# Strassen's seven products for four of eight projection kinds in a decoder layer on one core

## The chip, the cores and the metric

The kernel runs on one core of a Trainium2 chip. The metric is the device time of one execution in microseconds, the median of several runs. The core's engines are TensorE (PE, with its weight loads as PEld), VectorE (DVE), ScalarE (ACT), GpSimd (POOL) and SyncE (SP), which here only issues DMAs. Each engine works through its own queue in order and waits on semaphores for the others.

## The reference

One layer on L = 272 tokens (16 meta tokens ahead of 256), width 4096, all in float32:

```python
h = rmsnorm(x, norm_g)
p = h @ w_in                        # 4096 x 16384: eight kinds q k v g b c h z, 16 units of 128 columns each
o = stick_breaking_attention(q, k, v)             # 16 heads of 128, strictly causal
o = group_rmsnorm(o * silu(g), attn_norm_g, 16)   # norm over the 128 channels of a head
y = b * short_conv(c * h, conv_w)                 # width 3 along the tokens
y = group_rmsnorm(y * silu(z), conv_norm_g, 16)
x = x + concat([o, y]) @ w_out                    # 4096 x 4096
return rmsnorm(x, final_norm_g)[:, 16:]
```

A weight a(t, s) of the attention is sigmoid(z_ts) times the product of (1 - sigmoid(z_tj)) over s < j < t; it is computed in log space with a running sum along the keys.

## The kernel before, in words

All of w_in and w_out is read once, as 640 chunks of 128 x 1024 float32 (512 KB). Each chunk is split into two float32r parts, so that three products (high x low, high x high, low x high) make up for the short mantissa: `split` casts the chunk on ScalarE to `wh` (line 87) and subtracts on VectorE for `wl` (line 88). x comes transposed (`xt`), is scaled by norm_g and split in the same way into `xs` (`prep_x`, lines 190 and 191) and stays in SBUF, 32 slices of k with a high and a low part side by side. The factor 1/rms of each token is applied after the projection (`rstd`).

The projection works by channel: a block is 128 output columns of one kind and unit; its weights are held still in TensorE and the tokens stream. `mm_k` does one k of a block. For k, v, c and h it takes three matmuls of 272 or 258 columns (lines 227 to 229). For q, g, b and z, which need only the 256 real tokens, it takes one matmul of 256 columns with `wl` (line 221) and one of 512 with `wh`, high and low part of x side by side (line 223; line 220 is that for the first k); the two halves of the bank are added afterwards by `fold`.

The order of the work is written out by hand in `steps`: the first four blocks interleaved over k while x arrives (16 chunks), then block after block, heads and conv units in turn, four chunks a block; then the output projection by columns, each step two token tiles (`mm_out`, lines 476 to 478, the mixed channels held still and the weights streaming). The loop issues loads four chunks ahead and splits three ahead (`LOADS, SPLITS`). Everything else (scores, weights, transposes by 32 x 32 blocks, the short convolution, SiLU, the group norm with its matmul by ones on lines 281 and 282, `norm_b`) is put on a list by `later` and issued a few steps behind its block. The mixed channels stay in SBUF, already split, from the end of a unit on. Each PSUM tile is a bank of a pool of eight.

Of the kernel before, what the change touches and what calls it, by code (L numbers as in the profile page):

```python
# [8 lines left out]
F32 = mybir.dt.float32  # L9
# [6 lines left out]
P = 128  # L16
D = 4096
# [4 lines left out]
XROW = 320  # L22
HEADS = 16
UNITS = 32
EPS = 1e-6
# [11 lines left out]
S0 = 7  # L37
# [6 lines left out]
def kernel(ctx, tc, xt, xin, par, fg, w1, w2, out):  # L44
    nc = tc.nc

    const = ctx.enter_context(tc.tile_pool(name="const", bufs=1))
    wp = ctx.enter_context(tc.tile_pool(name="wp", bufs=4))
    wk = ctx.enter_context(tc.tile_pool(name="wk", bufs=1))

    wp.tile([P, 16], F32, name="pad_w", bufs=1)
    pp = ctx.enter_context(tc.tile_pool(name="pp", bufs=8, space=bass.MemoryType.PSUM))

    def bank(nm):
        return pp.tile([P, 512], F32, tag="bank", name=nm)


    ones = const.tile([P, P], F32, name="ones")
# [9 lines left out]
    raws, splits = {}, {}  # L68

    def load(ci, parts=1):  # L70
        t = wp.tile([P, 1024], F32, tag="raw", name=f"raw{ci}", bufs=4)
        n = 1024 // parts
        for i in range(parts):
            nc.sync.dma_start(out=t[:, i * n:(i + 1) * n], in_=src_of(ci)[:, i * n:(i + 1) * n])
        raws[ci] = t

    def split(ci, parts=1):
        t = raws.pop(ci)
        if ci in keep:
            h, lo = keep[ci]  # L80
        else:
            h = wp.tile([P, 1024], F32R, tag="wh", name=f"wh{ci}", bufs=4)
            lo = wp.tile([P, 1024], F32R, tag="wl", name=f"wl{ci}", bufs=4)
        n = 1024 // parts
        for i in range(parts):
            c = slice(i * n, (i + 1) * n)
            nc.scalar.copy(out=h[:, c], in_=t[:, c])  # L87
            nc.vector.tensor_tensor(out=lo[:, c], in0=t[:, c], in1=h[:, c].bitcast(F32), op=ALU.subtract)  # L88
        splits[ci] = (h, lo)


    ones_r = const.tile([P, P], F32R, name="ones_r")
    nc.scalar.copy(out=ones_r, in_=ones)


    za = const.tile([P, 3 * P + 64], F32, name="za")
    nc.vector.memset(za[:, 3 * P:], 0.0)

    at = const.tile([P, META + 3 * P], F32, name="at")
    nc.vector.memset(at[:, :META], 0.0)  # L100
    vt = const.tile([P, L + META], F32, name="vt")
    nc.vector.memset(vt[:, L:], 0.0)
    zmask = const.tile([P, ZW], F32, name="zmask")
    nc.vector.memset(zmask, 0.0)
    for off in (META, 144 + META + P):

        nc.gpsimd.affine_select(out=zmask[:, off:off + P], in_=zmask[:, off:off + P],
                                pattern=[[-1, P]], compare_op=ALU.is_gt, fill=NEG,
                                base=0, channel_multiplier=1)
    one = const.tile([P, 1], F32, name="one")  # L110
    nc.vector.memset(one, 1.0)
    gsc = const.tile([P, 32], F32, name="gsc")
    nc.vector.tensor_scalar(out=gsc, in0=pt[:, AG0:AG0 + 32], scalar1=RS, scalar2=None, op0=ALU.mult)
    rstd = const.tile([P, L], F32, name="rstd")

    def rsqrt_raw(src, n, eps, nm):

        x = wk.tile([P, 272], F32, tag="rx", name=f"rx{nm}", bufs=1)[:, :n]
        y = wk.tile([P, 272], F32, tag="ry", name=f"ry{nm}", bufs=1)[:, :n]
        t = wk.tile([P, 272], F32, tag="rt", name=f"rt{nm}", bufs=1)[:, :n]  # L120
# [12 lines left out]


    mixh, mixl = [], []

    def open_mix():
        sctx.close()
        mixp = ctx.enter_context(tc.tile_pool(name="mixp", bufs=1))
        mixp.tile([P, 24], F32, name="pad_m")  # L140
        mixh.extend(mixp.tile([P, SEQ], F32R, name=f"mixh{m}") for m in range(UNITS))
        mixl.extend(mixp.tile([P, SEQ], F32R, name=f"mixl{m}") for m in range(UNITS))

    steps = [(0, kc) for kc in range(16)]
    for b in range(4, 128):
        steps.extend((b, kc) for kc in range(4))
    n1 = len(steps)

    for nb in range(7):
        steps.extend((128 + nb, kc) for kc in range(16))
    for nb in (7, 8):
        steps.extend((128 + nb, kc) for kc in range(8))
    n_steps = len(steps)
    keep = {}

    def src_of(ci):
        return w1[ci] if ci < n1 else w2[ci - n1]

    LOADS, SPLITS = 4, 3
    tasks = []

    def later(at, fn):
        tasks.append((at, fn))

    def run_tasks(i):
        ready = [t for t in tasks if t[0] <= i]
        for t in ready:
            tasks.remove(t)  # L170
        for t in ready:
            t[1]()
# [7 lines left out]
    xr = [sp.tile([P, 4, L], F32, name=f"xr{j}") for j in range(8)]  # L180
    xsum = sp.tile([P, L], F32, name="xsum")

    def load_x(k, n):
        j, kk = k // 4, k % 4
        nc.sync.dma_start(out=xr[j][:, kk:kk + n, :], in_=xt[:, k:k + n, :])

    def prep_x(k):
        j, kk = k // 4, k % 4
        g = pt[:, G0 + k:G0 + k + 1]
        nc.scalar.mul(out=xs[j][:, kk, 0, :L], in_=xr[j][:, kk, :], mul=g)  # L190
        nc.vector.scalar_tensor_tensor(out=xs[j][:, kk, 1, :L], in0=xr[j][:, kk, :], scalar=g,
                                       in1=xs[j][:, kk, 0, :L].bitcast(F32),
                                       op0=ALU.mult, op1=ALU.subtract)

    def stat_x(j):
        tc.keep_in_program_order(nc.scalar.square(out=xr[j], in_=xr[j]))
        xq = sp.tile([P, L], F32, tag="xq", name=f"xq{j}", bufs=2) if j else xsum
        tc.keep_in_program_order(
            nc.vector.tensor_reduce(out=xq, in_=xr[j].rearrange("p k t -> p t k"), axis=AX.X, op=ALU.add))
        if j:  # L200
            nc.vector.tensor_tensor(out=xsum, in0=xsum, in1=xq, op=ALU.add)

    def finish_stats():
        ss = bank("ss_x")
        nc.tensor.matmul(out=ss[:, :L], lhsT=ones, rhs=xsum, start=True, stop=True)
        xm = wk.tile([P, 272], F32, tag="sg", name="xm")
        nc.vector.tensor_scalar(out=xm, in0=ss[:, :L], scalar1=1.0 / 32.0, scalar2=None, op0=ALU.mult)
        u = rsqrt_raw(xm, L, EPS, "x")
        nc.vector.tensor_scalar(out=rstd, in0=u, scalar1=RS, scalar2=None, op0=ALU.mult)
# [3 lines left out]
    def mm_k(b, k, h, lo):  # L213

        ps = psum[b]
        x = xs[k // 4][:, k % 4, :, :L]
        first, last = k == 0, k == KC - 1
        if b % 8 in (0, 3, 6, 7):
            if first:
                nc.tensor.matmul(out=ps, lhsT=h, rhs=x[:, :, META:], start=True, stop=False)  # L220
            nc.tensor.matmul(out=ps[:, :SEQ], lhsT=lo, rhs=x[:, 0, META:], start=False, stop=False)  # L221
            if not first:
                nc.tensor.matmul(out=ps, lhsT=h, rhs=x[:, :, META:], start=False, stop=last)  # L223
        else:
            s = 0 if b % 8 < 4 else META - 2
            o = ps[:, s:L]
            nc.tensor.matmul(out=o, lhsT=h, rhs=x[:, 0, s:], start=first, stop=False)  # L227
            nc.tensor.matmul(out=o, lhsT=h, rhs=x[:, 1, s:], start=False, stop=False)  # L228
            nc.tensor.matmul(out=o, lhsT=lo, rhs=x[:, 0, s:], start=False, stop=last)  # L229

    def mm_in(ci):
        b, kc = steps[ci]
        wh, wl = splits.pop(ci)
        if kc == 0:
            for bb in range(b, b + 4 if b == 0 else b + 1):
                psum[bb] = bank(f"mm{bb}")
        for kk in range(8):
            h = wh[:, kk * P:(kk + 1) * P]
            lo = wl[:, kk * P:(kk + 1) * P]
            if b == 0:  # L240
                mm_k(kk % 4, 2 * kc + kk // 4, h, lo)
            else:
                mm_k(b, kc * 8 + kk, h, lo)

    def blocks(dst, src, n):

        d = dst.rearrange("p (c x) -> p c x", c=n)
        s = src.rearrange("p (c x) -> p c x", c=n)
        for i in range(4):
            for j in range(4):  # L250
                o = d[32 * j:32 * j + 32, :, 32 * i:32 * i + 32]
                x = s[32 * i:32 * i + 32, :, 32 * j:32 * j + 32]
                if (i + j) % 2:
                    nc.vector.tensor_copy(out=o, in_=x)
                else:
                    nc.scalar.copy(out=o, in_=x)  # L256

    def fold(ps, r, nm, tag, width=SEQ):

        t = wk.tile([P, width], F32, tag=tag, name=f"{tag}{nm}")[:, :SEQ]  # L260
        nc.scalar.copy(out=t, in_=ps[:, SEQ:])
# [376 lines left out]
```

## Time and profile before

| | us |
|---|---|
| median of 3 runs | 1874.1 (1874.07 to 1874.17) |
| the profiled execution | 1873.31 |
| its span, first to last instruction | 1871.5 |
| granted TensorE clock in it | 0.998 |
| PE / DVE / ACT / POOL busy | 1859.1 / 1224.7 / 953.6 / 0.7 |

Busy time is the union of an engine's instructions. A row of a group reads: line, engine, operation, what is written and read, shapes, count | total busy us, mean ns of one | idle us of the engine just before them, and what ended that idle time. TensorE's matmuls overlap, so their means are longer than the distance from one to the next. A row of the timeline reads: start us, duration us, engine, line, operation. A row of the stretches gives for each engine its busy us with the count of instructions, then the granted clock, the DMA share and GB/s. A row of the waits reads: who waited for whom, us in total, times, longest us.

### The profile page before, as it was taken

How to read it: one execution, taken by the hardware profiler on the slowest of the kernel's cores; microseconds unless marked ns; L12 is line 12 of the kernel's file. 1: busy time of each engine (PE TensorE's matmuls, PEld its weight loads, DVE VectorE, ACT ScalarE, POOL GpSimd, SP SyncE). 2: the span in 40 equal slices, each digit the busy share in tenths (PEclk: the TensorE clock that was granted, in tenths of full speed). 3: DMA queues.
4: the chain of work that ended last, by engine and by line, in shares of the span. 5: the costliest groups of instructions: out<-in, count | busy, mean ns of one | idle time of the engine just before them, and what ended most of it. 6: DMA issues, size and time to landing. Idle time of an engine off the chain costs nothing.

```text
span 1871.5 us, 30516 instructions
## 1 busy us (share of the span) xinstructions
PE 1859.1 (99%) x12214; PEld 1707.0 (91%) x12214; DVE 1224.7 (65%) x1904; ACT 953.6 (51%) x1381; POOL 0.7 (0%) x6
## 2 busy tenths in 40 slices
PE   9999999999999999999999999999999999999997
PEld 8999999999999999999999999999999988888887
DVE  8987676767676767676767676767676765555544
ACT  7665555545454545454545454545454544444443
POOL 0000000000000000000000000000000000000000
PEclk9999999999999999999999999999999999999999
DMA  8555555555555555555555555555555586566564
GB/s 310 179 182 181 177 184 175 186 172 189 171 188 172 186 174 184 177 183 178 181 180 181 180 181 180 181 180 180 181 179 182 175 285 207 198 197 200 198 201 162
DMA packets 100510, 352.53 MB, mean 188 GB/s; under 512 B 11280, under 2 KB 12560, under 8 KB 100368
## 3 DMA queue, kind: packets, MB, share of 16 engines
q1 hardware_dynamic: 100368, 350.59, 56.0%
q8 instruction: 95, 1.56, 0.3%
q14 instruction: 47, 0.39, 0.1%
HBM read 346.35 MB, written 4.19 MB: 187 GB/s over the span
## 4 chain that ended last, share of the span: by engine, by line
PE 99%; DMA 0%; DVE 0%; SPq 0%; ACT 0%; issue 0%; DVEq 0%; ACTq 0%
PE mm L223 25%; PE mm L227 13%; PE mm L229 13%; PE mm L228 13%; PE mm L221 13%; PE mo L478 6%; PE mo L477 6%; PE mo L476 6%; PE mm L220 1%; PE z L309 0%; PE po L371 0%; DMA raw<-w 0%; PE po L373 0%; PE po L372 0%; PE z L308 0%; PE ss L281 0%
## 5 line engine op out<-in xcount | busy, mean ns | idle before, releaser
L88 DVE TENSOR_TENSOR wl<-raw,wh 128x1024 fp32r<-128x1024 f32 (+1 forms) x638 | 777.6, 1219 | 439.0 <-ACT wh L87 436.5
L87 ACT CAST wh<-raw 128x1024 fp32r<-128x1024 f32 (+1 forms) x638 | 668.1, 1047 | 753.7 <-PE mm L228 289.5
L223 PE MATMUL mm<-xs,wh 128*128 128x512 f32 x1984 | 701.8, 397 | 0.0
L227 PE MATMUL mm<-xs,wh 128*128 128x258 f32 (+1 forms) x2048 | 586.6, 287 | 0.0
L228 PE MATMUL mm<-xs,wh 128*128 128x258 f32 (+1 forms) x2048 | 581.3, 284 | 0.0
L229 PE MATMUL mm<-xs,wl 128*128 128x258 f32 (+1 forms) x2048 | 581.0, 284 | 0.0
L221 PE MATMUL mm<-xs,wl 128*128 128x256 f32 x2048 | 563.5, 280 | 0.2 <-DVE wl L88 0.2
L223 PEld LDWEIGHTS mm<-xs,wh 128*128 128x128 f32 x1984 | 372.7, 188 | 86.3
L221 PEld LDWEIGHTS mm<-xs,wl 128*128 128x128 f32 x2048 | 386.3, 189 | 4.8 <-DVE wl L88 0.6
L228 PEld LDWEIGHTS mm<-xs,wh 128*128 128x128 f32 x2048 | 385.8, 188 | 2.8
L227 PEld LDWEIGHTS mm<-xs,wh 128*128 128x128 f32 x2048 | 385.7, 188 | 1.3 <-ACT wh L87 0.2
L229 PEld LDWEIGHTS mm<-xs,wl 128*128 128x128 f32 x2048 | 385.7, 188 | 0.2
L476 PE MATMUL mo<-wh,mixl 128*128 128x512 f32 (+1 forms) x544 | 201.5, 370 | 0.0
L478 PE MATMUL mo<-wl,mixh 128*128 128x512 f32 (+1 forms) x544 | 201.5, 370 | 0.0
L477 PE MATMUL mo<-wh,mixh 128*128 128x512 f32 (+1 forms) x544 | 201.5, 370 | 0.0
L477 PEld LDWEIGHTS mo<-wh,mixh 128*128 128x128 f32 x544 | 102.5, 188 | 17.6
L476 PEld LDWEIGHTS mo<-wh,mixl 128*128 128x128 f32 x544 | 102.5, 188 | 17.5
L478 PEld LDWEIGHTS mo<-wl,mixh 128*128 128x128 f32 x544 | 102.5, 188 | 17.3
L256 ACT COPY at<-ya 32x96 f32<-32x96 f32 x128 | 34.5, 269 | 12.2 <-DVE ya L337 10.7
L256 ACT COPY vv<-yv 32x64 f32<-32x64 f32 x128 | 31.1, 243 | 1.7
L122 DVE TENSOR_SCALAR rxm<-ss 128x256 f32<-128x256 f32 x32 | 13.6, 424 | 25.6 <-PE ss L282 25.6
L323 DVE SCALAR_TENSOR_TENSOR zs<-zm,zl 128x416 f32<-128x416 f32 x16 | 9.5, 594 | 30.5 <-ACT zl L316 30.5
(141 smaller groups left out, 907.0 us busy)
## 6 DMA issues: line engine op xcount, KB each, us to landing
raw<-w SPq DMA_DIRECT2D x638, 512.0 KB, 3.3
xr<-xt SPq DMA_DIRECT2D x15, 272.0 KB, 6.2
res<-xin SPq DMA_DIRECT2D x14, 256.0 KB, 6.0
out<-res SPq DMA_DIRECT2D x4, 512.0 KB, 3.4
fg<-fg SPq DMA_DIRECT2D x7, 256.0 KB, 3.9
out<-res SPq DMA_DIRECT2D x2, 640.0 KB, 4.9
raw<-w SPq DMA_DIRECT2D x4, 256.0 KB, 4.2
res<-xin SPq DMA_DIRECT2D x4, 128.0 KB, 3.9
```

Source lines behind the costliest of these rows:

```text
L87: nc.scalar.copy(out=h[:, c], in_=t[:, c])
L88: nc.vector.tensor_tensor(out=lo[:, c], in0=t[:, c], in1=h[:, c].bitcast(F32), op=ALU.subtract)
L220: nc.tensor.matmul(out=ps, lhsT=h, rhs=x[:, :, META:], start=True, stop=False)
L221: nc.tensor.matmul(out=ps[:, :SEQ], lhsT=lo, rhs=x[:, 0, META:], start=False, stop=False)
L223: nc.tensor.matmul(out=ps, lhsT=h, rhs=x[:, :, META:], start=False, stop=last)
L227: nc.tensor.matmul(out=o, lhsT=h, rhs=x[:, 0, s:], start=first, stop=False)
L228: nc.tensor.matmul(out=o, lhsT=h, rhs=x[:, 1, s:], start=False, stop=False)
L229: nc.tensor.matmul(out=o, lhsT=lo, rhs=x[:, 0, s:], start=False, stop=last)
L256: nc.scalar.copy(out=o, in_=x)
L476: nc.tensor.matmul(out=o, lhsT=ml, rhs=h, start=m == 0, stop=False)
L477: nc.tensor.matmul(out=o, lhsT=mh, rhs=h, start=False, stop=False)
L478: nc.tensor.matmul(out=o, lhsT=mh, rhs=lo, start=False, stop=m == UNITS - 1)
```

## The change: what it does

- **Kinds and groups.** The 16 units of heads and the 16 of conv are worked in 8 groups of two each. k, v, c and h ("plain" blocks) are worked as before, by channel. q, g, b and z of a group, 8 blocks or 1024 columns, are worked by token: 128 tokens are held still and 512 columns of weights stream. For each pair of k slices they are one 2 x 2 x 2 block product: two token tiles, two k, two column halves (q and g; b and z).
- **Seven products.** Strassen's scheme in Winograd's form: seven products of 128 tokens x 512 columns for eight, each still three matmuls for the split. The sums of x for it (four tiles of 128 x 128 per pair of k) are made once by GpSimd, split and kept in SBUF (`S`). The sums of the weights (T and U, 128 x 1024 each) are made by GpSimd for every pair of k of every group, then split by ScalarE and VectorE like a loaded chunk. The chunks A and B hold the raw weights of a pair of k, arranged by the host. Seven banks gather the products over 16 pairs of k; the eighth, bank 7, serves plain blocks, scores, transposes and the rest in turn.
- **Order.** A piece list: 16 pieces of the first stage (k, v, c, h of unit 0), then for each group 16 times A, B, plain pieces (one in group 0, two later), T, U. In group 0 nine more pieces reload x by token for the statistics.
- **By token.** q is turned back by a TensorE transpose for the scores. SiLU, gates and the group norm work by token, with one factor per token and unit in place of a matmul by ones; the mixed channels are then transposed by TensorE.
- **Mixed channels in DRAM.** Groups 0 to 6 write them to DRAM by DMAs from ScalarE's queue; seven pieces "m" read and split them around the start of the output projection. The output projection itself is unchanged.

The diff, cut to its core:

```diff
+    for j in range(KC // 2):
+        pieces.append(("s", j))
+        ...
+        for j, ps in enumerate(counts):
+            pieces.append(("A", g, j))
+            pieces.append(("B", g, j))
+            for blk, kc in ps:
+                pieces.append(("p", blk, kc))
+                ...
+            pieces.append(("T", g, j))
+            pieces.append(("U", g, j))
+            if g == 0 and j < 7:
+                for q in {2: (2, 3), 4: (5, 6)}.get(j, (j + (j > 2) + (j > 4),)):
+                    pieces.append(("x", q))
+    ...
+    for nb in range(9):
+        for kc in range(16 if nb < 7 else 8):
+            pieces.append(("o", nb, kc))
+            if nb == 0 and kc % 2 == 0 and 2 + kc // 2 < GROUPS - 1:
+                pieces.append(ms[2 + kc // 2])
+    def prep_x(j, parts=1):
+        ...
+        f = wk.tile([P, 4, P], F32, tag="u2", name=f"sf{j}", bufs=2)
+        v = nc.gpsimd
+        v.tensor_tensor(out=f[:, 0, :], in0=a21, in1=a22, op=ALU.add)
+        v.tensor_tensor(out=f[:, 2, :], in0=a11, in1=a21, op=ALU.subtract)
+        v.tensor_tensor(out=f[:, 1, :], in0=f[:, 0, :], in1=a11, op=ALU.subtract)
+        v.tensor_tensor(out=f[:, 3, :], in0=a12, in1=f[:, 1, :], op=ALU.subtract)
+    def sum_t(g, j, a, b):
+        t = wp.tile([P, 1024], F32, tag="tt", name=f"t{g}_{j}", bufs=2)
+        nc.gpsimd.tensor_tensor(out=t[:, :512], in0=a[:, :512], in1=b[:, 512:], op=ALU.subtract)
+        nc.gpsimd.tensor_tensor(out=t[:, 512:], in0=a[:, 512:], in1=b[:, 512:], op=ALU.subtract)
+    def sum_u(g, j, a, b, t):
+        u = wp.tile([P, 1024], F32, tag="tt", name=f"u{g}_{j}", bufs=2)
+        nc.gpsimd.tensor_tensor(out=u[:, 512:], in0=a[:, 512:], in1=t[:, :512], op=ALU.add)
+        nc.gpsimd.tensor_tensor(out=u[:, :512], in0=u[:, 512:], in1=b[:, :512], op=ALU.subtract)
+    def mm_p(i, j, a, h, lo):
+        o = psum["P", j]
+        nc.tensor.matmul(out=o, lhsT=a[1], rhs=h, start=first, stop=False)
+        nc.tensor.matmul(out=o, lhsT=a[0], rhs=h, start=False, stop=False)
+        nc.tensor.matmul(out=o, lhsT=a[0], rhs=lo, start=False, stop=final)
+        work = {"A": ((1, a(0, 0), lo_), (3, s(4), hi_)), "B": ((2, a(0, 1), lo_),),
+                "T": ((5, s(1), lo_), (7, s(3), hi_)), "U": ((4, a(1, 1), lo_), (6, s(2), hi_))}[p[0]]
+    def evict_3(g):
+        V.tensor_tensor(out=cq[:, 1], in0=psum["P", 6], in1=cq[:, 1], op=ALU.add)
+        V.tensor_tensor(out=u, in0=psum["P", 6], in1=u, op=ALU.add)
+        V.scalar_tensor_tensor(out=u, in0=psum["P", 5], scalar=-1.0, in1=u, op0=ALU.mult, op1=ALU.add)
+        ...
+    def silu(g, q):
+        for t in range(2):
+            A.activation(out=s[:, t], in_=z[:, t], func=AF.Sigmoid, scale=rt[:, t:t + 1])
+            G.tensor_tensor(out=z[:, t], in0=z[:, t], in1=s[:, t], op=ALU.mult)
+    def norm(g, q):
+        for t in range(2):
+            for u in range(2):
+                A.activation(out=j, in_=y[:, t, u], func=AF.Square, scale=(rt if q == "h" else rt2)[:, t:t + 1],
+                             accum_out=ss[:, 2 * u + t:2 * u + t + 1])
+        ...
+    def mix_t(g, q, u, o):
+        for t in range(2):
+            T.transpose(out=o[:, t * P:(t + 1) * P], in_=y[:, t, u], identity=ident)
+    def mix_out(g, q, us, o):
+        ...
+            if g < GROUPS - 1:
+                m = wk.tile([P, SEQ], F32, tag="u2", name=f"mf{q}{g}_{u}", bufs=2)
+                A.mul(out=m, in_=p, mul=gn)
+                A.dma_start(out=mixd[g][:, m0 + u, :], in_=m)
```

More of the change, by code (lines that the diff above doesn't have):

```diff
@@ L92 @@
[L92 to L103, printed above, removed]
+    pieces = []
+    ends = {}
+    fin = {}
+    for j in range(KC // 2):
+        pieces.append(("s", j))
@@ new lines @@
+    last = ("p", (UNITS_PER - 1, 0))
+    ms = [("m", g) for g in range(GROUPS - 1)]
+    pieces += [last + (0,), last + (1,), last + (2,), ms[0], last + (3,), ms[1]]
+    ends[GROUPS - 1].append(len(pieces) - 2)
+    n1 = len(pieces)
+    for nb in range(9):
[3 more added lines that the diff above has]
+                pieces.append(ms[2 + kc // 2])
+    n = len(pieces)
+    where, c1, c2 = {}, 0, 0
@@ L132, in rsqrt_raw, with small @@
         return y
[L135 to L172, printed above, removed]
+    def small(nm):
+        return [wk.tile([P, 4], F32, tag=f"sm{i}", name=f"{nm}{i}") for i in range(3)]
     xctx = ExitStack()
@@ L211 @@
-    psum = {}
[L213 to L243, printed above, removed]
+    S = [sp.tile([P, 2, 4, P], F32R, name=f"sum{j}") for j in range(16)]
@@ new lines, in prep_s, with open_mix @@
+    def prep_s(j, f):
+        nc.scalar.copy(out=S[j][:, 0], in_=f)
+        nc.vector.tensor_tensor(out=S[j][:, 1], in0=f, in1=S[j][:, 0].bitcast(F32), op=ALU.subtract)
+    mixh, mixl = [], []
+    def open_mix():
+        sctx.close()
+        mixp = ctx.enter_context(tc.tile_pool(name="mixp", bufs=1))
+        mixh.extend(mixp.tile([P, 4, SEQ], F32R, name=f"mixh{g}") for g in range(GROUPS))
+        mixl.extend(mixp.tile([P, 4, SEQ], F32R, name=f"mixl{g}") for g in range(GROUPS))
+    raws, splits, keep = {}, {}, {}
@@ new lines, in load @@
+    def load(i):
+        p = pieces[i]
+        if p[0] in "TU":
+            return
+        if p[0] == "s" and p[1] > 0:
+            load_x(p[1])
+        t = wp.tile([P, 1024], F32, tag="raw", name=f"raw{i}", bufs=5)
+        raws[i] = t
+        if p[0] == "x":
+            if p[1] < 8:
+                r, c = divmod(p[1], 4)
+                nc.sync.dma_start(out=t, in_=xin[r * P:(r + 1) * P, c * 1024:(c + 1) * 1024])
+            else:
+                nc.sync.dma_start(out=t[:, :512], in_=xm)
+        elif p[0] == "m":
+            nc.sync.dma_start(out=t.rearrange("p (a b) -> p a b", a=4), in_=mixd[p[1]])
+        elif i < 2:
+            for h in range(2):
+                nc.sync.dma_start(out=t[:, 512 * h:512 * h + 512], in_=where[i][:, 512 * h:512 * h + 512])
+                if i == 0 and h == 0:
+                    nc.sync.dma_start(out=xr[0][:, 1:, :], in_=xt[:, 1:2, :])
+        else:
+            nc.sync.dma_start(out=t, in_=where[i])
```

853 lines of the change are left out of this document (535 added, 318 removed).

## The prediction, made before the change was run

> **What bounds the kernel now.** I read the page first (engine shares, slices, chain), then the groups by shape, then the timeline of TensorE for the spacing of its matmuls, then the waits.
>
> ```profile
> span 1871.5 us, 30516 instructions
> PE 1859.1 (99%) x12214; PEld 1707.0 (91%) x12214; DVE 1224.7 (65%) x1904; ACT 953.6 (51%) x1381; POOL 0.7 (0%) x6
> ...
> PEclk9999999999999999999999999999999999999999
> ```
> ```profile
> by line: PE mm L223 24.7%; PE mm L227 13.4%; PE mm L229 13.2%; PE mm L228 13.2%; PE mm L221 12.8%; PE mo L478 6.3%; PE mo L477 6.3%; PE mo L476 6.2%; PE mm L220 0.8%; PE z L309 0.4%; PE po L371 0.4%; DMA raw<-w 0.3%; PE po L373 0.3%; PE po
> ```
>
> The chain that ended last is TensorE almost from end to end, at full clock. Lines 220, 221 and 223 are the blocks q, g, b and z: 24.7 + 0.8 + 12.8 = 38.3%, so 717 us of the 1871.5. Lines 227 to 229 are k, v, c and h (39.8%), lines 476 to 478 the output projection. Whatever shortens TensorE's work shortens the kernel, until another engine is later.
>
> ```profile
> L223 PE MATMUL mm<-xs,wh 128*128 128x512 f32 x1984 | 701.8, 397 | 0.0
> ```
> ```profile
> 289.92 0.40 PE L223 MATMUL mm<-xs,wh 128*128 128x512 f32 x1
> ...
> 298.40 0.40 PE L223 MATMUL mm<-xs,wh 128*128 128x512 f32 x1
> ```
> ```profile
> 308.04 0.28 PE L227 MATMUL mm<-xs,wh 128*128 128x272 f32 x1
> ...
> 311.74 0.28 PE L227 MATMUL mm<-xs,wh 128*128 128x272 f32 x1
> ```
> ```profile
> 1600.09 0.39 PE L476 MATMUL mo<-wh,mixl 128*128 128x512 f32 x1
> ...
> 1602.81 0.39 PE L476 MATMUL mo<-wh,mixl 128*128 128x512 f32 x1
> ```
>
> The mean of one matmul (397 ns) is no price, since they overlap; the price is the spacing of starts. Between the first pair of rows lie 24 pairs (one of 256 columns, one of 512): 8.48 / 24 = 0.353 us a pair. Between the second lie 30 matmuls of 272 columns: 3.70 / 30 = 0.123 us. Between the third lie 12 of 512 columns, with 128 columns of tokens held still and weights streaming: 2.72 / 12 = 0.227 us. That third form is the one the new products have.
>
> **The change: TensorE.** Before, each of 64 blocks takes 32 pairs: 2048 pairs, the 717 us above (0.353 x 2048 = 723 agrees). After, 8 groups x 16 pairs of k x 7 products x 3 matmuls = 2688 matmuls of 512 columns in the third form: 2688 x 0.227 = 609 us. That is 108 us off, more than an eighth, since the form is also denser than the old pair. k, v, c and h keep their 6144 matmuls, and the output projection is the same.
>
> ```profile
> 318.19 0.24 PE z L308 x2
> 318.44 0.46 PE z L309 x2
> 344.68 0.43 PE po L371 x2
> 345.11 0.25 PE po L372 x2
> 345.36 0.32 PE po L373 x2
> ```
> ```profile
> 300.04 0.28 PE L281 MATMUL ss<-yh,ones_r 128*128 128x256 f32 x1
> ...
> 300.16 0.28 PE L282 MATMUL ss<-yh,ones_r 128*128 128x256 f32 x1
> ```
>
> The norm by token needs no matmul with ones: 64 of them, at the 0.12 us of the last two rows, are 8 us off. Working by token costs transposes instead: per group 4 for q, 4 for the conv, 8 for the mixed channels, 128 in all, each float32 on 128 columns. No transpose is in this trace. The nearest row is line 308, float32 on 144 columns in 0.24 us, so 0.21 us for 128 and 27 us in all; the low end is half of a 256-column matmul, 0.06 us and 8 us, the high end the 0.32 us of line 373, a small one by itself, and 41 us. I take 27, the same number format. [...] The head's output is 5 float32 matmuls of 128 columns, 1.07 us, for the 1.00 us of lines 371 to 373: 1 us over 16 heads. The scores stay.
>
> TensorE's sum: -108 - 8 + 27 + 1 = -88 us, so 1784 if it stays as full as now.
>
> **The change: what must hide.** In groups 1 to 6 one pair of k ("a step" below) is pieces A, B, two plain ones, T and U. TensorE: 21 x 0.227 + 48 x 0.123 = 10.7 us, and with 0.4 us for its share of scores and transposes 11.1 us.
>
> ```profile
> L88 DVE TENSOR_TENSOR wl<-raw,wh 128x1024 fp32r<-128x1024 f32 x634 | 774.9, 1222 | 438.5 <-ACT wh L87 436.1
> L87 ACT CAST wh<-raw 128x1024 fp32r<-128x1024 f32 x634 | 665.7, 1050 | 753.2 <-PE mm L228 289.5 <-PE mm L223 210.7 <-PE mo L477 166.0
> L316 ACT ACT_TABLE_LOAD x16 | 20.5, 1283 | 0.3
> L315 ACT ACTIVATE zl<-zl 128x416 f32<-128x416 f32 x16 | 8.9, 553 | 0.5
> L316 ACT ACTIVATE zl<-zl,half 128x416 f32<-128x416 f32 x16 | 10.3, 644 | 0.2
> L486 ACT ACTIVATE junk<-y 128x512 f32<-128x512 f32 x14 | 8.4, 598 | 9.3 <-DVE y L484 9.3
> L484 DVE TENSOR_TENSOR y<-mo,res 128x512 f32<-128x512 f32 x14 | 9.6, 684 | 0.0
> L323 DVE SCALAR_TENSOR_TENSOR zs<-zm,zl 128x416 f32<-128x416 f32 x16 | 9.5, 594 | 30.5 <-ACT zl L316 30.5
> L325 DVE TENSOR_TENSOR_SCAN zl<-one,zs 128x272 f32<-128x272 f32 x16 | 11.2, 700 | 0.0
> L123 DVE TENSOR_SCALAR rym<-rxm 128x256 int32<-128x256 int32 x32 | 9.2, 289 | 0.6
> L107 POOL TENSOR_SCALAR_AFFINE_SELECT zmask<-zmask 128x128 f32<-128x128 f32 x2 | 0.5, 292 | 1.2 <-DVE half L433 1.2
> ```
>
> The sums T and U must be split like raw weights, so a step splits five pieces of 1024 and one of 512 where TensorE's time was four before. VectorE: 5 x 1.222 + 0.684 = 6.8 us; ScalarE: 5 x 1.050 + 0.598 = 5.8 us. Both lie under 11.1 us. VectorE's other work falls (nine passes of 256 columns in each norm become passes of 4 columns) and gains six evictions of 512 columns per group, 6 x 0.684 = 4.1 us. With some 30 us of head and conv work in a group (16 steps), 2 us a step, it is at about 8.8 of 11.1 us.
>
> GpSimd now makes T and U: four sums of 512 columns a step. Its only row with data is line 107, 128 columns with one input in 0.292 us. Linear in columns that is 1.17 us for 512; the low end is VectorE's own 0.684, the high end 2.34 us, if the second input doubles it. I take 1.17, its own engine's row: 4.7 us a step, and SiLU and conv products (4 + 2 of 256 columns, 4 of 128 in a group, 4.7 us) add 0.3. Even the high end, 10.0 us, lies under 11.1, so GpSimd by itself costs nothing.
>
> SyncE's queue issues four loads a step, none for T and U, and nothing else passes them but x and the mixed channels, which stand in the order of the pieces.
>
> ```profile
> 0.00:55.00 55.00, 53.55 (x354) 49.70 (x355) 47.97 (x70) 42.01 (x63) 0.74 (x6) 1.00 0.82 297
> ...
> 200.00:400.00 200.00, 200.00 (x1394) 186.80 (x1393) 133.91 (x219) 102.01 (x151) 0.00 (x0) 1.00 0.54 180
> ```
> ```profile
> ACT wh L87 <- PE mm L228: 289.5, 171, 2.1
> ```
>
> The last two columns of the stretches are the DMA share and GB/s. A step of groups 1 to 6 loads 2 MB (four pieces) in 11.1 us, 189 GB/s, as now. Group 0 has one plain piece a step (4.8 + 3.0 = 7.7 us) and, for its first seven, a rereading of x for the statistics: 4.3 pieces of 0.52 MB, 292 GB/s. The start of the output projection reads the mixed channels back, one piece to two of weights: about 300 GB/s for 38 us. The start of before moved 297 GB/s with TensorE 97% busy, so this is just carried; I add 4 us (0 to 20). The mixed channels' writes, 28 of 128 KB on ScalarE's queue, are seven pieces' worth over the whole span: nothing.
>
> Four places where TensorE may wait:
> - The first stage (16 pieces of 24 x 0.123 = 2.95 us). VectorE now has there a scale (0.29), a subtraction of 544 columns (about 0.72), one of 512 (0.68) and one of 1024 (1.22): 2.9 us, ScalarE 2.7, one chain through GpSimd between them, and x in two buffers for all 16 loads, with each load queued ahead of the weights in SyncE's queue. That is no slack at all: 0.5 us a piece, 8 us (0 to 30).
> - The end of each group: 4.1 us of evictions after U, while the next A, B and a plain piece give TensorE 5.0 us. Then the next split is about 1 us late: 8 us in all (0 to 16).
> - Bank 7, one bank for all plain blocks, scores, transposes and heads, which each wait for the eviction before. Between such a use and the next plain block lie A and B, 2.0 us, against an eviction of some 0.6 us: nothing, as long as ScalarE is free.
> - The lead of the splits. The wait in the last fence says ScalarE splits only when TensorE gives a buffer free, three pieces ahead: 3 x 2.95 = 8.8 us now, but U, A and B only 3.4 us, of which cast and subtraction take 2.3. A wait of over 1.1 us on either engine is seen by TensorE: 2 us here, and a rival below.
>
> Sum: 1784 + 4 + 8 + 8 + 2 = 1806 us of span. The profiled execution of before took 1873.31 us for a span of 1871.5, and the runs' median is 1874.1: 2.6 us more. **1809 us**, 3.5% faster; own range 1780 to 1838, by the ends given (transposes -19 / +14, first stage -8 / +22, DMA -4 / +16, group ends -8 / +8, not all at once).
>
> **The rivals.** First, GpSimd and VectorE hinder each other (slower). If a GpSimd sum and a VectorE operation with two SBUF inputs cannot run at once, their times add: per step 6.8 us of splits, 0.5 us of the heads' work (rows of lines 323 and 325 and their like, some 3.7 us a head, 7.4 us in 16 steps), and 4.7 + 0.3 of GpSimd: 12.3 us against 11.1. That is +1.2 us in 112 steps, 134 us; in group 0, 5.6 + 5.0 = 10.6 against 7.7, 46 us; in the first stage 2.6 + 4 x 0.29 = 3.8 against 2.95, 14 us. In all 194 us, about 2000 us. With p the price of one sum of 512 columns, this extra is 546p - 445 us; it eats the 66 us of gain at p = 0.94 us, and decides from there on. If the two hinder each other for part of the time only, it lies between: I put this case at 1940. For it: both engines' loads are large and steady in every step. Against it: no row shows it, since GpSimd never works beside VectorE before, and it needs p above 0.94 as well. [...]
>
> Second, the small pieces starve TensorE (still faster). Pieces of 0.7 and 1.4 us with a lead of three, and scores, weights and norms in the same ScalarE and VectorE queues: a table load and three passes of the scores take ScalarE 1.28 + 0.55 + 0.55 + 0.64 = 3.0 us, against 1.1 us of slack. Two waits of about 1 us for each of 16 heads and 8 groups are 40 to 50 us: about 1850. Against it: VectorE's 65% and ScalarE's 51% leave idle time, and casts could go ahead of the scores.
>
> Third, the four edges cost nothing and transposes are cheap: 1785 us or below.
>
> **How the numbers follow.** The forecast of 1809 with its range has 0.53, the starved pieces 0.12, the cheap one 0.07, GpSimd against VectorE 0.28, of which 0.02 ends within 0.2% of before and some 0.12 above 1940. 0.2% (3.7 us) is about what this measurement can tell. Faster 0.71, same 0.02, slower 0.27. The range reaches from 1780 to 1940: it leaves out some 0.05 below and 0.12 above.
>
> **What would show it.** Right: TensorE busy at 97% or more; 0.227 us between the new products' starts; GpSimd at 40 to 50%; line 88's counterpart still at 1.22 us for 1024 columns. The first rival would show as that operation stretched well above 1.22 us, GpSimd's sums well above 1.2, VectorE near 100%, and TensorE waiting for split T and U pieces. The second: TensorE waiting on casts behind scores and norms, clustered at each head. A slow first stage: the first 50 us drawn out, TensorE waiting for the first splits and x. What would make me wrong is above all p and the shared use of SBUF, of which this trace says nothing.

## The result and the profile after

The changed kernel takes 2145.8 us (2142.83 to 2147.06, four runs) against 1874.1 us: 1.1447 times as long, interval 1.1427 to 1.1467. The forecast was 1809 us, with 1780 to 1940 as its range: wrong in sign, and outside the range. Other medians below stand against 1874 us on the same chip; `e3` and `v1` were run four times, every other experiment once.

The head of the page of the kernel after, and its slices of granted clock:

```profile
span 2143.9 us, 29926 instructions
PE 1901.1 (89%) x10938; PEld 1664.1 (78%) x10938; DVE 1691.1 (79%) x1877; ACT 1176.1 (55%) x1784; POOL 1034.1 (48%) x696
...
PEclk8999999999999999999999999899999999999999
```

TensorE was busy 99% of the span and is now at 89%; VectorE went from 65% to 79%, GpSimd from nothing to 48%. Neither looks full. That is the trap of this profile, and the groups show why, by shape (row of VectorE's subtraction, GpSimd's four sums, and the small copies of a head):

```profile
L325 DVE TENSOR_TENSOR wl<-raw,wh 128x1024 fp32r<-128x1024 f32 x506 | 715.3, 1423 | 263.7 <-ACT wh L324 258.3 <-DMA raw<-w 1.5 <-PE s L339 0.3
L278 POOL TENSOR_TENSOR t<-raw,raw 128x512 f32<-128x512 f32 x128 | 263.1, 2055 | 581.2 <-DVE wl L325 548.6 <-DMA raw<-w 26.7 <-DVE rt L181 3.3
L279 POOL TENSOR_TENSOR t<-raw,raw 128x512 f32<-128x512 f32 x128 | 234.5, 1832 | 0.0
L285 POOL TENSOR_TENSOR u<-raw,t 128x512 f32<-128x512 f32 x128 | 216.1, 1689 | 3.0 <-DVE wl L325 3.0
L286 POOL TENSOR_TENSOR u<-u,raw 128x512 f32<-128x512 f32 x128 | 213.0, 1664 | 10.0
L438 DVE COPY at<-ya 32x96 f32<-32x96 f32 x128 | 86.1, 672 | 2.0
```

The split of 1024 columns went from 1222 to 1423 ns in the mean, the 32 x 96 copies from 217 (line 254 of before) to 672 ns. A GpSimd sum lasts 1.28 us at its shortest (line 278 by its source line, min/median/max in ns) and 2.2 in the median:

```profile
L278 POOL TENSOR_TENSOR t<-raw,raw x128: 1275/2208/3348, 62.3 to 1732.1; 128x512 f32<-128x512 f32 x128
```

The timeline at the start of group 4, GpSimd and VectorE, shows what happens between them (start, duration):

```profile
928.69 1.78 POOL L278 TENSOR_TENSOR t<-raw,raw 128x512 f32<-128x512 f32 x1 [1.72 <-DMA raw<-w]
930.43 1.26 POOL L279 TENSOR_TENSOR t<-raw,raw 128x512 f32<-128x512 f32 x1
931.65 1.26 POOL L285 TENSOR_TENSOR u<-raw,t 128x512 f32<-128x512 f32 x1
932.98 1.27 POOL L286 TENSOR_TENSOR u<-u,raw 128x512 f32<-128x512 f32 x1
```
```profile
928.09 1.23 DVE L325 TENSOR_TENSOR wl<-u,wh 128x1024 fp32r<-128x1024 f32 x1 [0.88 <-ACT wh L324]
929.23 1.26 DVE L178 TENSOR_SCALAR nc<-nc 128x4 int32<-128x4 int32 x1
930.53 1.18 DVE L180 TENSOR_TENSOR nc<-nc 128x4 f32<-128x4 f32 x1
931.74 1.18 DVE L181 TENSOR_TENSOR nc<-nc,nc 128x4 f32<-128x4 f32 x1
932.96 0.16 DVE L182 SCALAR_TENSOR_TENSOR nc<-nc,nc 128x4 f32<-128x4 f32 x1
933.16 1.11 DVE L183 SCALAR_TENSOR_TENSOR nc<-nc 128x4 f32<-128x4 f32 x1
935.33 0.15 DVE L184 TENSOR_TENSOR nc<-nc,nc 128x4 f32<-128x4 f32 x1
935.98 0.42 DVE L474 TENSOR_TENSOR cc<-mm,rstd 128x258 f32<-128x258 f32 x1
```

The first sum begins inside a split and lasts 1.78 us; the next three take 1.26. VectorE's operations on four columns, 0.16 us when nothing is in the way, last 1.11 to 1.26, and each of those ends within 0.02 us of a sum's end (929.23 + 1.26 and 928.69 + 1.78; 930.53 + 1.18 and 930.43 + 1.26): it waits out a whole sum. One at most slips in between two sums, and the next waits again. In this stretch VectorE's busy time is nearly all waiting. So the busy shares of the two count the same time twice: from 300 to 1700 us, by the records of both, VectorE works 1181 us and GpSimd 803, but one or the other works in 1321 of the 1400 us, 94% (in before 67% from 300 to 1500 us, VectorE alone). By their undisturbed durations a group holds 138 us of VectorE's own work (the run without sums, below), 64 sums x 1.27 = 81 and 9 of products: 228 us, where a group takes 215 and TensorE needs 178.

Not all of VectorE's work is held. An operation that reads a PSUM bank lasts as long with sums beside it (fourteen of these fifteen ran wholly beside one in after) as in `e8`, which has no sums:

```profile
L454 DVE TENSOR_TENSOR vt<-mm,rstd 128x272 f32<-128x272 f32 x15 | 6.6, 441 | 1.5 <-PE mm L340 1.2
```
```profile
L452 DVE TENSOR_TENSOR vt<-mm,rstd 128x272 f32<-128x272 f32 x15 | 6.6, 442 | 11.3 <-PE mm L338 11.3
```

A transpose of 32 x 32 blocks is not held either (467 ns against 472). About 13 of the 138 us are of these two kinds; the other 125, with 81 and 9, come to the 215 us that a group takes. The sum is good to some per cent only, since one or the other works in 94% of the time and not in all of it.

What is behind waits in turn. ScalarE and TensorE at the same place:

```profile
936.10 1.28 ACT L588 ACTIVATE cb<-cb,ssc 128x128 f32<-128x128 f32 x4 [7.10 <-DVE ssc L585]
```
```profile
936.46 1.11 PE L618 MATMUL qT<-ident,cq 128*128 128x128 f32 x4 [5.90 <-DVE cc L474]
937.22 0.78 PE L346 MATMUL P<-wh,xs 128*128 128x512 f32 x1
937.80 0.63 PE L347 MATMUL P<-wh,xs 128*128 128x512 f32 x1
938.22 0.63 PE L348 MATMUL P<-wl,xs 128*128 128x512 f32 x1
938.65 0.63 PE L346 MATMUL P<-wh,sum 128*128 128x512 f32 x1
...
939.65 0.39 PE L346 MATMUL P<-wh,xs 128*128 128x512 f32 x1
939.88 0.40 PE L347 MATMUL P<-wh,xs 128*128 128x512 f32 x1
```

TensorE waits 5.9 us for bank 7, because c's eviction (line 474) stands behind the norm in VectorE's queue. Then, for some 2 us, its products start 0.42 us apart instead of 0.23; the granted clock is 0.53 from 936.3 to 939.5 us and 1.00 from 939.7 on.

From all of TensorE's rows, taking the usual distance to the next start (0.227 us at 512 columns, 0.123, 0.118 and 0.117 at 272, 258 and 256): usual distances sum to 1779 us, distances of about double length add 80, waits 273, start and tail the rest. TensorE's own work is about what was predicted. The waits are what was not.

### The profile page after: what moved, and what is told of

It is laid out like the page before. It is cut to its first block, busy times and chain, and to the rows that moved or that the text cites. A ratio compares the mean times of both kernels' runs of the same rounds, so it can differ in the third digit from the quotient of the medians.

```text
span 2143.9 us, 29926 instructions
## 1 busy us (share of the span) xinstructions
PE 1901.1 (89%) x10938; PEld 1664.1 (78%) x10938; DVE 1691.1 (79%) x1877; ACT 1176.1 (55%) x1784; POOL 1034.1 (48%) x696
## 5 line engine op out<-in xcount | busy, mean ns | idle before, releaser
L278 POOL TENSOR_TENSOR t<-raw,raw 128x512 f32<-128x512 f32 x128 | 263.1, 2055 | 581.2 <-DVE wl L325 548.6
L338 PEld LDWEIGHTS mm<-xs,wh 128*128 128x128 f32 x1920 | 369.6, 192 | 57.9 <-ACT wh L324 19.7
L340 PEld LDWEIGHTS mm<-xs,wl 128*128 128x128 f32 x1920 | 369.1, 192 | 46.6 <-DVE wl L325 46.3
L339 PEld LDWEIGHTS mm<-xs,wh 128*128 128x128 f32 x1920 | 371.3, 193 | 4.2
L279 POOL TENSOR_TENSOR t<-raw,raw 128x512 f32<-128x512 f32 x128 | 234.5, 1832 | 0.0
L286 POOL TENSOR_TENSOR u<-u,raw 128x512 f32<-128x512 f32 x128 | 213.0, 1664 | 10.0
L285 POOL TENSOR_TENSOR u<-raw,t 128x512 f32<-128x512 f32 x128 | 216.1, 1689 | 3.0 <-DVE wl L325 3.0
L346 PE MATMUL P<-wh,sum 128*128 128x512 f32 x512 | 208.9, 408 | 0.0
L347 PE MATMUL P<-wh,sum 128*128 128x512 f32 x512 | 206.7, 404 | 0.0
L348 PE MATMUL P<-wl,sum 128*128 128x512 f32 x512 | 205.6, 402 | 0.0
L325 DVE TENSOR_TENSOR wl<-t,wh 128x1024 fp32r<-128x1024 f32 x128 | 170.3, 1330 | 42.6 <-ACT wh L324 42.2
L348 PE MATMUL P<-wl,xs 128*128 128x512 f32 x384 | 165.2, 430 | 38.7 <-DVE wl L325 38.4
L325 DVE TENSOR_TENSOR wl<-u,wh 128x1024 fp32r<-128x1024 f32 x128 | 171.1, 1336 | 12.1 <-ACT wh L324 10.6
```

The costliest lines, as they stand in the source:

```text
L278: nc.gpsimd.tensor_tensor(out=t[:, :512], in0=a[:, :512], in1=b[:, 512:], op=ALU.subtract)
L279: nc.gpsimd.tensor_tensor(out=t[:, 512:], in0=a[:, 512:], in1=b[:, 512:], op=ALU.subtract)
L285: nc.gpsimd.tensor_tensor(out=u[:, 512:], in0=a[:, 512:], in1=t[:, :512], op=ALU.add)
L338: nc.tensor.matmul(out=o, lhsT=h, rhs=x[:, 0, s:], start=k == 0, stop=False)
L348: nc.tensor.matmul(out=o, lhsT=a[0], rhs=lo, start=False, stop=final)
```

## The experiments

They fall into three questions: is it GpSimd's sums; by what means; and where the rest is.

**Is it the sums?** `e1` has none:

```diff
-            tt = sum_t(p[1], p[2], a, t)
-            sums[("T",) + p[1:]] = tt
-            sums[("U",) + p[1:]] = sum_u(p[1], p[2], a, t, tt)
+            sums[("T",) + p[1:]] = fixed[0]      # two tiles filled once
+            sums[("U",) + p[1:]] = fixed[1]
```

> Leaves out GpSimd's four sums per step: T and U are two fixed tiles, written once, so q, g, b and z are not the reference's. Splits, matmuls, loads and every other queue stay. Theory A (GpSimd's reads of SBUF and VectorE's operations with two SBUF inputs or in a fast mode exclude each other for whole instructions): 1810 to 1850 us, TensorE's own work of 1782 us plus the slow first stage, which still has its GpSimd sums; the split of 1024 columns back at 1.22 us, the norm's operations on 4 columns at 0.16. Theory B (short pieces with a lead of three, one bank for everything, ScalarE and VectorE in order): 2050 us or more, since all of that stays.

Measured 1892.5 us, 253 less, though 42 above theory A's range. Head of its page and its split:

```profile
PE 1821.6 (96%) x10938; PEld 1628.6 (86%) x10938; DVE 1338.4 (71%) x1879; ACT 1172.7 (62%) x1784; POOL 119.2 (6%) x184
```
```profile
L327 DVE TENSOR_TENSOR wl<-raw,wh 128x1024 fp32r<-128x1024 f32 x506 | 619.9, 1229 | 322.2 <-ACT wh L326 319.1 <-PE P L350 0.8 <-PE P L349 0.5
```

The split is back at 1229 ns. The weights' sums cost 253 us. But 1892 is still slower than before: the rest is looked for below.

**By what means?** A sum could cost as one more link between load and split, by writing to SBUF, or by reading it. `e2` keeps writes and most of the busy time and drops the reads; its fills do not wait for A and B as the sums do, so the link from load to split is kept in `e3` alone, which makes the sums on VectorE:

```diff
-        nc.gpsimd.tensor_tensor(out=t[:, :512], in0=a[:, :512], in1=b[:, 512:], op=ALU.subtract)
+        for _ in range(2):                                  # e2, and so for all four
+            nc.gpsimd.memset(t[:, :512], 0.01)
+        nc.vector.tensor_tensor(out=t[:, :512], ...)        # e3, and so for all four
```

> In place of each GpSimd sum stand two fills of the same 512 columns with a constant, so GpSimd keeps its place in the chain (it waits for the buffers and the splits of T and U wait for it) and is busy about 4 us a step, but reads nothing there; q, g, b and z are not the reference's. Theory A with reads as the shared thing: 1810 to 1870 us, like the run without sums. Theory A with any use of the port, writes too: near 2100. Theory C (what is late is GpSimd's link in the chain, not a port): 2100 or more.

> The four sums per step on VectorE in place of GpSimd, all results kept. Theory A: VectorE gains 4 x 0.69 us a step and loses every wait for GpSimd; 8.8 + 2.7 = 11.5 us against TensorE's 11.1, so 1850 to 1920 us. Theory B: VectorE has more in its queue than before and is late more often: 2150 to 2250.

`e2` took 1907.6 us, 38 above the range for reads alone and far below the others, and `e3` 1925.3 (1.0274 times before, 1.0257 to 1.0291), 5 above its range. Of their groups, `e2`'s fills of u and one of `e3`'s four sums:

```profile
L288 POOL MEMSET u<- 128x512 f32 x512 | 250.7, 533 | 1.1 <-DVE wl L327 1.1
```
```profile
L286 DVE TENSOR_TENSOR u<-u,raw 128x512 f32<-128x512 f32 x128 | 88.0, 687 | 0.7
```

With 500 us of GpSimd's writes (the same again for t) the kernel loses 15 us over none, with 927 us of its reading sums (263 + 235 + 216 + 213) 253. And the same sums in VectorE's own queue, 0.69 us each, cost only 33: one engine doing both, one after the other, is 220 us faster than two sharing them. So reading is in, and neither the link (in `e3`) nor writing (in `e2`) explains 253 us. Writing is not quite free: in `e2` a copy of 32 x 96 lasts 394 ns in the mean for 217, so a fill holds copies too, while the split of 1024 columns stays at 1229.

GpSimd also stood idle 549 us of after until VectorE gave a buffer of T or U free (row of line 278 above). More of these buffers were not tried.

**How long is the hold?** `e5` makes T in one sum of 1024 columns instead of two of 512; `e4` takes the nine operations on four columns out of the norm by token:

```diff
-        (T's two sums)
+        nc.gpsimd.tensor_tensor(out=t.rearrange("p (a b) -> p a b", a=2), in0=a.rearrange("p (a b) -> p a b", a=2),
+                                in1=b[:, None, 512:].broadcast_to([P, 2, 512]), op=ALU.subtract)     # e5
```
```diff
-        r = rsqrt_raw(ss, 4, EPS, *small(f"n{q}{g}_"))
-        V.tensor_tensor(out=ss, in0=r, in1=fac[:, f:f + 4], op=ALU.mult)
+        V.tensor_tensor(out=ss, in0=ss, in1=fac[:, f:f + 4], op=ALU.mult)     # e4
```

> The two GpSimd sums that make T become one of 1024 columns (the same work in one instruction); results kept. Theory A with a hold for the whole instruction: the sum takes about 2.5 us where nothing hinders it, and an operation of 4 columns on VectorE that meets it can now last up to 2.5 us where 1.28 was the longest; the time moves little, 2120 to 2200 us. If the port were granted piece by piece, the small operations would stay at or below 1.3 us.

> Leaves out the chain of nine operations on 4 columns for the reciprocal root in the group norm, 16 times (the norm's factor is wrong); GpSimd's sums stay. Theory A: each of these operations waits for the end of a GpSimd sum (1.2 us for 0.16), so 16 x 6 to 9 us of VectorE go, and with them the waits of TensorE for late evictions of the one shared bank: 2050 to 2090 us. If the stretched splits alone matter: 2130 to 2146.

`e5`: 2142.5 us, no change in the time, but in the hold. One four-column operation by its source line (min/median/max ns), in after, `e5` and `e3`:

```profile
L183 DVE SCALAR_TENSOR_TENSOR nc<-nc x8: 164/1111/1261, 284.2 to 1778.2; 128x4 f32<-128x4 f32 x8
```
```profile
L183 DVE SCALAR_TENSOR_TENSOR nc<-nc x8: 164/1113/2342, 281.8 to 1774.7; 128x4 f32<-128x4 f32 x8
```
```profile
L183 DVE SCALAR_TENSOR_TENSOR nc<-nc x8: 152/154/163, 255.4 to 1558.7; 128x4 f32<-128x4 f32 x8
```

The longest hold grows with the sum, from 1.26 to 2.34 us, and is gone where GpSimd sums nothing. The 2.34 us are one operation, the only one of the eight that met T's wide sum, and it ends within 0.02 us of that sum's end: VectorE is held for a whole instruction, not slowed. One input is enough to be held: line 178 in the rows above lasted 1.26 us (0.17 at its shortest in after), and the copies of 32 x 96 went from 217 to 672 ns. That two inputs or a fast mode decide, as theory A has it, was its author's supposition; no run shows it.

`e4`: 2098.2 us, 48 less, for 144 operations that are 23 us of undisturbed work (0.16 each). That lies between the two ranges, 8 us from the one in which these holds matter.

**Are VectorE and GpSimd full together, or does each sum cost by what it holds up?** `e11` leaves T to a filled tile and keeps U's two sums (with one buffer for U):

```diff
-            tt = sum_t(p[1], p[2], a, t)
+            tt = fixed
```

> Leaves out T's two GpSimd sums in every pair of k (T is a tile filled once); U's two sums stay, from the same chunks, and x's sums too. Two ways in which the weights' sums could cost their 254 us (2146 with all four, 1892 with none). If VectorE and GpSimd share one reading path and together are full, the cost is not proportional: a group of after has 138 us of VectorE's own work (from the run without any sums), 64 sums x 1.27 = 81 us and 9 us of products, 228 us against a group of 215; with half the sums it is 138 + 41 + 9 = 188 us, which lies at the 186 us that a group takes without sums, so nearly all of the cost goes: about 1900 to 1940 us, VectorE or GpSimd busy in clearly under 96% of a group. If instead each sum costs by what it holds up at the head of VectorE's queue, half the sums cost half: about 2019 us (1990 to 2050), groups of some 200 us.

1948.0 us: 8 above the one range, 42 below the other. The first half of the sums costs 56 us, the second 198. So the cost grows as for a resource that fills up. But by the sum above half of it is 125 + 41 + 9 = 175 us a group, just under TensorE's 178, and 56 us are paid all the same: a part is paid before the two are full (one or the other works in 91% of the time from 300 to 1500 us). That this part is what a sum holds up in a queue on which TensorE waits is likely and not shown. `e10` asks the same of the kernel before, which has a lead of three full pieces: one GpSimd subtraction of 512 columns, read by nobody, per chunk of the projection, 512 in all as in after.

```diff
+            j = wp.tile([P, 512], F32, tag="gj", bufs=1)
+            nc.gpsimd.tensor_tensor(out=j, in0=t[:, :512], in1=t[:, 512:], op=ALU.subtract)
```

> The kernel before with one thing added: for each chunk of the input projection GpSimd subtracts one half of the raw chunk from the other into a tile that nobody reads, 512 sums of 512 columns, the same number as the change has and at nearly the same density (one per 2.9 us). Results kept. Theory A: the splits beside them are stretched from 1.22 towards 1.4 us on average, the sums from 1.28 to 1.7; VectorE's 65% and the sums' 44% come to more than the time, so 1900 to 1990 us. Theories B and C, which blame the new order and its dependencies: 1872 to 1880, since nothing waits for these sums but a raw buffer.

1902.7 us, 29 more. Its groups and the projection after the first 200 us (busy us of PE, PEld, DVE, ACT, POOL, then clock, DMA share, GB/s):

```profile
L91 DVE TENSOR_TENSOR wl<-raw,wh 128x1024 fp32r<-128x1024 f32 x634 | 932.5, 1485 | 171.3 <-ACT wh L90 169.6
L81 POOL TENSOR_TENSOR gj<-raw 128x512 f32<-128x512 f32 x512 | 842.1, 1645 | 683.5 <-DMA raw<-w 676.7
```
```profile
200.00:1500.00 1300.00, 1298.67 (x9025) 1211.97 (x9024) 1226.74 (x1415) 669.79 (x1015) 720.15 (x441) 1.00 0.55 179
```

The same hold (1485 for 1222 ns). But the loss lies at the start: matmul for matmul, TensorE is 27.6 us behind before at 235 us and 29.4 at the end. From 200 to 1500 us it waits for next to nothing, though VectorE or GpSimd works in 98% of that time. Before's VectorE had about 780 us of work there on SBUF alone; with 441 x 1.27 = 560 it comes to 1340 us in 1300. So in `e10` two engines that are just full together cost next to nothing where nothing waits for the sums (1298.67 of 1300 us busy on TensorE), and the first 200 us, where VectorE was busier (162 us in before), pay. In after the two are over TensorE's time by a fifth (215 for 178), since the change had already filled VectorE with five and a half splits a step for four; there the splits of T and U also wait for the sums, which `e10` leaves out as well.

**Where is the rest?** `e6` makes the first stage's four small sums one fill (`nc.gpsimd.memset(f, 0.5)`), and `e8` is `e1` and `e6` together: GpSimd reads no weights and no x. `e9` is `e8` with a longer lead (`LOADS, SPLITS = 6, 4`, five buffers of `wh` and `wl`, four of `raw`).

> In the first stage GpSimd's four sums of x per piece are replaced by one fill with a constant, which reads nothing (the products are not the reference's); all else stays. Theory A: the first product starts at 62 to 68 us of the span in place of 81, VectorE's subtraction of 544 columns falls from 1.00 to about 0.72 us; the whole is 15 to 20 us shorter. Theory D (x in two buffers, loads queued ahead of the weights): it stays at 75 us or more.

> Both left out, the weights' sums (fixed tiles) and the first stage's sums of x (one fill per piece), so that GpSimd reads nothing but in the few products of each group. Theory A: the two savings add, 1892 - 21 = 1871 us, with the first product at 60 us. What is then above TensorE's own 1782 us has nothing to do with GpSimd's sums and is theory B's. If the first stage is late for another reason as well: 1885 or more.

> The same without any sums, and splits issued four pieces ahead in place of three (five buffers for the split parts, four for raw weights, loads six pieces ahead). Theory B with the lead as the cause: most of TensorE's 9 us of waits and slow clock in each group go, 1810 to 1845 us. Theory E (the one shared bank and the order in the queues, whatever the lead): 1860 to 1875.

`e6`: 2125.1 us, 21 less, all of it in the first stage (81 to 60 us). The subtraction there, in after and `e6`:

```profile
L223 DVE TENSOR_TENSOR xs<-xr,xs 128x544 fp32r<-128x544 f32 x15 | 15.0, 1000 | 2.5 <-ACT xs L222 2.5
```
```profile
L223 DVE TENSOR_TENSOR xs<-xr,xs 128x544 fp32r<-128x544 f32 x15 | 11.1, 737 | 1.2 <-ACT xs L222 1.2
```

`e8`: 1870.9 us. The two add up (1892 - 21 = 1871). `e9`: 1865.6, so the lead of the splits is worth 5 us, about the spread of repeated runs of one kernel (4 us in after). One group of after and one of `e8`:

```profile
688.00:903.00 215.00, 190.10 (x1149) 168.35 (x1148) 179.70 (x195) 123.09 (x192) 122.87 (x78) 0.94 0.48 159
```
```profile
565.00:750.00 185.00, 180.46 (x1149) 163.96 (x1148) 137.84 (x195) 122.31 (x192) 8.89 (x14) 0.99 0.56 185
```

Without any sum, `e8` still has 60 us of waits and 25 of double distances beside 1772 of usual ones. That is as long as before: the seven products' gain is gone even when the sums are free.

**A better version?** `e7` is `e3` with SiLU's and the conv's products on VectorE too, so GpSimd reads next to nothing. `v1` is `e7` with T in one operation, the 32 x 32 block copies all on ScalarE, and the sums of x split one piece later:

```diff
-            G.tensor_tensor(out=z[:, t], in0=z[:, t], in1=s[:, t], op=ALU.mult)
+            V.tensor_tensor(out=z[:, t], in0=z[:, t], in1=s[:, t], op=ALU.mult)     # e7, v1
...
-                if (i + j) % 2:
-                    V.tensor_copy(out=o, in_=x)
-                else:
-                    A.copy(out=o, in_=x)
+                A.copy(out=o, in_=x)                                                # v1
```

> The kernel with the sums on VectorE, and also SiLU's and the conv's products of each group on VectorE, so that GpSimd does nothing but fills after the first stage. Theory A: the eight group starts, where these products still stretch copies and splits, give back 1 to 3 us each: 1900 to 1917 us. Theory B (VectorE is simply too full, 84%): 3.7 us more a group on it, 1925 to 1950.

> The same, and VectorE relieved: T in one operation of 1024 columns, the 32 x 32 block copies all on ScalarE, and in the first stage the split of a piece's x sums issued one piece later, so that ScalarE does not wait for GpSimd at the head of its queue. Theory A: VectorE about 11 us a group lighter, the first stage 8 to 12 us shorter: 1860 to 1895 us. Theory B (the lead of three pieces and the one shared bank): 1900 or more.

`e7` took 1919.4 us, 6 less than `e3`. `v1` took 1926.6 (1.0282 times before, 1.0264 to 1.0299), 32 above the range hoped for. The copies that left VectorE's queue stand in ScalarE's, sixteen in a row for 4.5 us where there were eight. TensorE's waits for ScalarE's eviction of bank 7, 1.6 us in `e7`, are now (total, times, longest):

```profile
PE mm L341 <- ACT mfc L605: 17.3, 14, 1.4
```

In half of the cases the eviction stands right behind copies; in the other half ScalarE itself waits for VectorE there (14.5 us, 7 times), whose splits come after the late casts.

So no version with all the work in it beat the kernel before.

## Why the prediction was wrong, point by point

- **TensorE's sum, 1784 us: nearly right, with two terms off.** In `e8`, span less waits and double distances is 1869 - 60 - 25 = 1784; the same figure for before is about 1860, so the gain is some 76 us of the forecast 88. The new products start 0.231 us apart in the mean of their usual distances, for 0.227: 11 us more. The transposes start 0.11 us apart in `e8`, for 0.21: about 12 us for all 128, and not 27. One lasts 272 ns (line 594 of after, `mx`, the mean of 32), but they overlap, and the distance is the price. (The four of q from 936.46 to 937.22 above, 0.19 us each, were at half pace.) The rest of the difference was not traced.
- **"GpSimd by itself costs nothing": the step that failed.** It compared GpSimd's 4.7 us a step, and VectorE's 8.8, each with TensorE's 11.1. VectorE's figure was right (138 / 16 = 8.6 in `e8`). But the part of it that works on SBUF alone, 7.8 us, did not run beside the sums, so the comparison had to be with 7.8 + 4 x 1.27 + 0.6 of products = 13.4 us a step, well over 11.1, and a step did take 215 / 16 = 13.4. In all the weights' sums cost 253 us.
- **The first rival was the case**, and had 0.28 instead of most of the chance. Its formula with the measured p = 1.27 gives 546 x 1.27 - 445 = 248 us, against 253 + 21 measured. That it comes so near is in part luck: it counts no copies, and the measured cost holds some 55 us of slow pace after waits (80 - 25) that it does not know. It failed in two choices: p was put at 1.17 (it is 1.27 alone), and it was marked down to 1940 for hindering "part of the time only", where the hold is for whole instructions (2.34 us to the end of the one wide sum met in `e5`) and hits copies with one input too (672 ns for 217). Its sign "VectorE near 100%" was also the wrong one to name: VectorE shows 79%. The time in which one or the other works shows the fill (94%), but not the cost by itself, as the 98% of `e10` say.
- **The first stage, +8 us (0 to 30):** the first of the new products started at 81 us; `e6`'s 60 gives 21 to GpSimd's sums there, where the formula had 14.
- **Group ends, bank 7 and lead, 10 us together: too little.** `e8`, free of sums, ends 62 us above the forecast: these terms and the first stage's, with 4 for DMA, came to 22 us; the waits and double distances of `e8` are 85. The second rival's 1850 for small pieces lay nearer the size, and its mechanism, casts behind other work in ScalarE's queue, shows in `e8`. Near the start of a group the norm's first square waits 5 us for GpSimd's product (`cb`, line 569), and a cast for which TensorE waits stands behind it:

```profile
765.67 0.40 ACT L579 ACTIVATE jc<-cb,rt 128x128 f32<-128x128 f32 x1 [5.07 <-POOL cb L569]
...
766.07 1.03 ACT L322 CAST wh<-raw 128x1024 fp32r<-128x1024 f32 x1
```
```profile
767.15 0.39 PE L336 MATMUL mm<-xs,wh 128*128 128x258 f32 x1 [2.38 <-ACT wh L322]
```

Of the waits that the views list for TensorE, 37 us in `e8` are for casts and splits of weights and 2 for bank 7 and the work on it. With the longer lead of `e9` they are 20 and 18: one takes the place of the other, and the time moved by 5 us. Bank 7, priced at nothing, also cost 83 us in after, where the transposes of q and of the conv and the head's product wait for evictions by the held VectorE (36.2 + 25.2 + 21.2). More buffers for both at once were not tried.
- **DMA, +4 us:** the stage of the output projection took 363.7 us in after and 363.9 in `e8`, with 7 us of waits on TensorE in all, against 351 in before; part of the 12 us is work of the last group done within it. No run separated the term; it is too small to matter.

## What to carry to other kernels

In this kernel, work of GpSimd that reads SBUF did not run beside VectorE's work on SBUF but was added to it (125 + 81 + 9 = 215 us, the time of a group); only what reads PSUM (441 ns for 442), and the transposes (467 for 472), ran beside it. So compare the sum of both with the bound, by undisturbed durations, and where it clearly exceeds the bound put the work on the engine that does it fastest (here VectorE, 0.69 against 1.27 us a sum). In a profile, look at how far the same operation's mean moved and at minimum against median, not at the busy shares, since an operation that is held counts as busy. And a gain on TensorE that needs more splits, evictions and a shared bank in the same time is to be priced by the slack it uses up: here that alone ate 62 of 65 us.

## What was not expected of the hardware

- After the 5.9 us wait above TensorE ran at half pace for a while: products 0.42 us apart for some 2 us; such extra distance comes to 80 us in all of after (25 in `e8`). In after the granted clock is 0.50 in the 2 us behind each of the seven longest waits (5.7 to 5.9 us), but 1.00 behind the one of 3.06 us that ends at 1473.3 us. The mean granted clock is 0.951 in after and 0.987 in `e8`. So the longest waits cost more than their length, at which the prediction priced all of them.
- VectorE's smallest operations lose most where they meet a sum: 0.16 us becomes 1.1 to 1.3 beside sums of 512 columns, up to 2.3 beside one of 1024.
- GpSimd's fills hindered little beside copies (394 ns for 217): from 300 to 1500 us of `e2` they took 401 us, 284 of them while VectorE worked, and the whole kernel lost 15 us over `e1`.
- VectorE's operations that read PSUM were not held (442 ns of `vt<-mm,rstd` in `e8`, 441 beside sums), while splits (1423 ns for 1222), copies (672 for 217) and four-column operations (up to 1.26 us for 0.16) were.
